# A two-layer decoder trunk: the MLP's down phase in a fixed order, copies of the up seam on two engines, RWKV's v splits and scan load placed anew

## The chip, the cores and the metric

The kernel runs on one core of a Trainium2 chip. Its time is the device time of one execution in microseconds (us); three runs gave 2987.73 us at the median, 2983.43 to 2993.65. A profile is one further execution, recorded instruction by instruction. Engines are named as the profile names them: PE is TensorE (PEld its weight loads), DVE VectorE, ACT ScalarE, POOL GpSimd, SP SyncE, which here only issues transfers; SPq and POOLq are the queues on which SP and POOL issue them.

## What is computed

A trunk of two layers over 1024 tokens of width 1024, all in float32. Each layer has a token mixer (layer 0 a gated linear recurrence, layer 1 RWKV-7), a cross-attention into 256 memory tokens, and an MLP, each between RMS norms and added to the residual:

```python
for i in range(DEPTH):                      # DEPTH = 2
    hn = rms_norm(x, g[0])
    t = rglru_mixer(hn, ...) if i % 2 == 0 else rwkv7_mixer(hn, ...)
    x = x + rms_norm(t, g[1])
    c = mem_cross_attention(rms_norm(x, g[2]), mem_n, c_w_q[i], c_w_kv[i], c_w_o[i])
    x = x + rms_norm(c, g[3])
    m = sqrelu_mlp(rms_norm(x, g[4]), m_w_up[i], m_w_down[i])
    x = x + rms_norm(m, g[5])

def sqrelu_mlp(h, w_up, w_down):            # 1024 -> 4096 -> 1024
    return jnp.square(jax.nn.relu(h @ w_up)) @ w_down
```

In RWKV-7, `v = (x + xx * mu[3]) @ w_rkv[2]`, with `xx` the previous token less this one, is the last of the three large projections ahead of the scan over time; `g = sigmoid(xg @ g1) @ g2` is the gate.

## The kernel before

**Splits.** A float32 matrix enters TensorE as two parts, a high and a low one: ACT casts it (line 217), and DVE, or in places POOL, subtracts the cast from the value (line 218). `mm3` then issues three matmuls for one product: high by high, high by low, low by high (lines 318 to 320). A split of a 128 x 1024 tile is so one ACT and one DVE instruction, and the matmuls with a low operand wait for the second.

**The MLP by seven products.** Both of its multiplications are done in blocks of 2 x 2 with seven block products in place of eight; p1 to p7 are these products, t1 to t4 and s1 to s4 the sums of blocks that enter them.

**The up seam** is the place where the MLP begins. The last of eight token tiles gets its norm (lines 642, 643, 327, 331, 650), and `combine_in` transposes the tokens on TensorE (line 384), four 128 x 128 blocks into a bank of PSUM. ACT copies each bank out with the norm's gain (line 385), 16 copies a layer, in two halves of eight. DVE and POOL then form the sums t1, t2, t3, t4 (lines 405 to 412), and each is split. In `make` (line 449) the w tiles of the first up tiles are loaded and split between the last token tiles; `MAKE` says after which.

**The up phase** (`cphase`) runs over 16 w tiles, two at a time at the start and at the end (`together`). `take` gives out the next split tile of a plan; `depth` says how many are kept split ahead, `ahead` how many more are loaded. For the last tile both are 0. Behind p7 of the last pair the function `then` takes the down phase's first weights and first operands. The result of the up phase goes to DRAM (`spill`), as seven blocks and sums for each of four groups; POOL forms the sums (lines 960 to 963).

**The down phase** has four groups g of 1024 hidden units and seven steps in each, 28 in all. A step multiplies one block or sum of the spilled tokens (A, two tiles of 128 x 1024) with one of the weights (B, two tiles; the sums of these, DSUMS, are formed by POOL at line 445). In each step p goes over four banks with 12 matmuls each (48 a step), after which DVE adds the bank into the accumulator (line 1014), or ACT copies it in group 0. The next group's weights are taken at step 5 (`n == 5`). Where the splits of the next steps stand against these additions on DVE is not written down: `take` emits a split when `depth` allows, and the scheduler places it by its priority.

**RWKV v.** `fphase` goes over eight feature tiles f of v, the first two together. After each, `evac_v` copies v out of PSUM on ACT (line 1425), TensorE transposes it (1435), ACT copies the transposes (1436), and TensorE forms the bonus (1446) and the gate (the product with z). Weights for the next tile are split ahead by `take`. `early(f)` loads what evac_v needs (1459, 1461), and `load(0)`, emitted after f = 6 (`LD`), loads the operands of the scan's first steps (1484, 1488, 1490); the scheduler may issue it earlier. The scan begins with matmuls on v as read back from DRAM (lines 1506 and 1627).

Of the kernel before, what the change touches and what calls it, by code (L numbers as in the profile page):

```python
# [27 lines left out]
MAKE = (5, 6)  # L28
# [21 lines left out]
class Net:  # L50
    def __init__(self, ctx, tc, I, plan=None):
# [3 lines left out]
        self.raws, self.parts, self.rows = {}, {}, {}  # L55
        self.later, self.between = [], []
        self.made = {}
# [31 lines left out]
    @contextmanager  # L89
    def behind(self):  # L90

        with ExitStack() as stack:
            if not self.rec:
                last = {i.engine: i for i in self.nc.cur_bb.bb.instructions}
                for i in last.values():
                    stack.enter_context(self.tc.issue_after(i))
            yield

# [123 lines left out]
    def load(self, desc):  # L222
        kind, w = desc[0], desc[1]
        dma = self.nc.sync.dma_start
        if kind == "d":

            v = w.rearrange("(j e p) (n c) -> e n p j c", e=2, p=128, n=2)
            raw = {}
            for e, n in ((0, 0), (1, 0), (0, 1), (1, 1)):
                raw[e, n] = [self.unit() for _ in range(2)]  # L230
                for i, t in enumerate(raw[e, n]):
                    dma(t.rearrange("p (j c) -> p j c", j=2), v[e, n, :, 2 * i:2 * i + 2, :])
            return raw
        if kind == "a":
            two = [self.unit() for _ in range(2)]
            for i, t in enumerate(two):
                dma(t.rearrange("p (j c) -> p j c", j=2), self.spill[w][:, desc[2], 2 * i:2 * i + 2, :])
            return two
        if kind == "b":
            return None  # L240
# [21 lines left out]
    def take(self, desc):  # L262
        if self.rec:
            self.plan.append(desc)
            return Nothing() if desc[0] in "dab" else (Nothing(), Nothing())
        i = self.taken
        assert self.plan[i][0] == desc[0], (self.plan[i], desc)
        self.taken += 1
        while self.within(i, self.loaded, self.depth + self.ahead):
# [4 lines left out]
        return self.parts.pop(i)  # L274
# [5 lines left out]
    def advance(self, i):  # L280
        while self.split_done < self.loaded and self.within(i, self.split_done, self.depth):
# [5 lines left out]
            elif kind == "d":  # L287
                self.parts[j] = self.rows[self.plan[j][2]] = raw
            elif kind == "a":
                self.parts[j] = [self.split(t) for t in raw]  # L290
            elif kind == "b":
                self.parts[j] = self.combine_d(*self.plan[j][1:])
            else:
                self.parts[j] = self.split(raw)
# [78 lines left out]
    def combine_in(self, xs, hf, g, B):  # L373
# [3 lines left out]
        for k in range(KT):  # L377
# [7 lines left out]
            nc.scalar.activation(t[:, o], p, AF.Copy, scale=self.colt[:, g + k:g + k + 1])  # L385
# [52 lines left out]

    def combine_d(self, name, g):

        f = self.rows[g]
        if name in DSUMS:
            o, x, y = DSUMS[name]
            for i in range(2):
                self.nc.gpsimd.tensor_tensor(f[o][i], f[x][i], f[y][i], ALU.subtract)  # L445
            return [self.split(f[o][0]), self.split(f[o][1], eng=self.nc.gpsimd)]
        return [self.split(t) for t in f[{"b11": (0, 0), "b21": (1, 0), "b22": (1, 1)}[name]]]
# [13 lines left out]
    def cphase(self, w, n, B, func, evac, then, ahead=2):  # L461
# [58 lines left out]
        def together(two, mid=lambda: None):  # L520
            for i in two:
                if i == n - 1:

                    self.depth, self.ahead = 0, 0
                begin(i)
                finish(i)
            mid()
            for step in (p5, p6, p7, p3, p4):
                for i in two:
                    step(*st[i], i)  # L530
                if step is p7 and two[-1] == n - 1:
                    with self.behind():
                        then()
# [405 lines left out]
    def mlp(self, layer, xt, raw, post, late=None):  # L939
# [30 lines left out]
        W = lambda g: self.take(("d", down[g * 1024:g * 1024 + 1024, :], g))  # L970
        ops = []

        def then():

            self.depth, self.ahead = 0, 0
            W(0)
            ops.extend([self.take(("a", 0, 0)), self.take(("b", "b11", 0))])
            self.depth, self.ahead = DOWN

        rest = self.cphase(up, 16, xt, AF.Relu, out, then)  # L980
        acc = self.big((4, 1024))
        raw += [t.rearrange("p t (k c) -> p (t k) c", c=512) for t in acc]
        left, right = slice(0, 512), slice(512, 1024)

# [7 lines left out]
        for g in range(4):  # L992
            if late and g >= LATE:
                late.pop(0)()
            ps = {}
            for n, (name, qa, qb, bank, begins, ends, to) in enumerate(steps):
                if n == 5 and g < 3:
                    W(g + 1)
                A, B = (ops.pop(0), ops.pop(0)) if ops else (self.take(("a", g, qa)), self.take(("b", qb, g)))
                for p in range(4):  # L1000
                    if begins:
                        ps[bank, p] = self.bank(p + 1)
                    o = ps[bank, p]
                    for j in range(4):
                        at = slice((j % 2) * 512 + p * 128, (j % 2) * 512 + p * 128 + 128)
                        bt = slice((j % 2) * 512, (j % 2) * 512 + 512)
                        self.mm3(o, [t[:, at] for t in A[j // 2]], [t[:, bt] for t in B[j // 2]],
                                 begins and j == 0, ends and j == 3, skip_group_check=True)
# [6 lines left out]
                    if g == 3 and name == "p3":  # L1015
                        post(p, acc[0][:, p, :])
                    if g == 3 and name == "p7" and layer == 1 and p == 3:

                        sq = [self.small(1) for _ in range(2)]
# [708 lines left out]
```

## Time and profile before

| what | value |
|---|---|
| median of three runs | 2987.73 us |
| the profiled execution | 2991.93 us, its span 2990.2 us |
| PE busy | 2861.3 us (96% of the span) |
| DVE, ACT, POOL busy | 1812.9, 1355.9, 1166.1 us |
| mean granted TensorE clock | 0.983 of full |
| down phase, layer 0 | about 990 to 1334 us |
| up seams | 702 to 727 and 2353 to 2376 us |
| first v transposes | 1682.49 us |

A row of a timeline gives an instruction's start, its length, the engine, the line, the tiles (written<-read) and in square brackets how long the engine sat idle before it and what ended that. A row of the waits gives the waiting engine and line, what it waited for, the total, how often, and the longest. A row of a table of windows gives the stretch and its length, then the busy time of PE, PEld, DVE, ACT and POOL with the number of instructions, the granted clock (PEclk), the DMA share and GB/s.

### The profile page before, as it was taken

How to read it: one execution, taken by the hardware profiler on the slowest of the kernel's cores; microseconds unless marked ns; L12 is line 12 of the kernel's file. 1: busy time of each engine (PE TensorE's matmuls, PEld its weight loads, DVE VectorE, ACT ScalarE, POOL GpSimd, SP SyncE). 2: the span in 40 equal slices, each digit the busy share in tenths (PEclk: the TensorE clock that was granted, in tenths of full speed). 3: DMA queues.
4: the chain of work that ended last, by engine and by line, in shares of the span. 5: the costliest groups of instructions: out<-in, count | busy, mean ns of one | idle time of the engine just before them, and what ended most of it. 6: DMA issues, size and time to landing. Idle time of an engine off the chain costs nothing. (4 is left out here: it accounts for less than half of the span.)

```text
span 2990.2 us, 42725 instructions
## 1 busy us (share of the span) xinstructions
PE 2861.3 (96%) x16987; PEld 2381.1 (80%) x16987; DVE 1812.9 (61%) x2012; ACT 1355.9 (45%) x1975; POOL 1166.1 (39%) x1055
## 2 busy tenths in 40 slices
PE   7999999999999999999999898989999899999998
PEld 6888798887888878877777677878788788887886
DVE  5576552546455587867685526884354745558776
ACT  6464342536444543347452534442244644454332
POOL 2000110024766664431486215651001566667442
PEclk9999999999999999999999899999999999999999
DMA  8212262113444654332656889752312244455443
GB/s 256 74 50 86 97 200 72 57 71 99 158 155 154 223 201 144 119 113 101 175 163 181 223 246 225 175 131 92 99 53 82 89 147 151 153 210 199 162 137 120
DMA packets 382887, 421.91 MB, mean 141 GB/s; under 512 B 91248, under 2 KB 293216, under 8 KB 382688
## 3 DMA queue, kind: packets, MB, share of 16 engines
q1 hardware_dynamic: 370656, 379.19, 42.1%
q0 software_dynamic: 11568, 39.41, 3.6%
q8 instruction: 133, 2.18, 0.3%
q14 instruction: 66, 0.54, 0.1%
q10 hardware_dynamic: 464, 0.59, 0.1%
HBM read 284.31 MB, written 134.74 MB: 140 GB/s over the span
## 5 line engine op out<-in xcount | busy, mean ns | idle before, releaser
L218 DVE TENSOR_TENSOR u<-u,u 128x1024 fp32r<-128x1024 f32 (+1 forms) x518 | 813.0, 1595 | 366.4 <-ACT u L217 331.7
L217 ACT CAST u<-u 128x1024 fp32r<-128x1024 f32 (+1 forms) x550 | 542.8, 1023 | 372.7 <-PE q L319 139.6
L319 PE MATMUL q<-u,u 128*128 128x512 f32 (+2 forms) x1824 | 699.8, 385 | 12.4 <-DVE u L218 12.1
L318 PE MATMUL q<-u,u 128*128 128x512 f32 (+2 forms) x1824 | 696.6, 386 | 12.9 <-DVE z L1014 8.2
L320 PE MATMUL q<-u,u 128*128 128x512 f32 (+2 forms) x1824 | 694.3, 384 | 1.1 <-DVE u L218 1.1
L318 PE MATMUL p<-u,u 128*128 128x512 f32 (+1 forms) x1728 | 658.6, 384 | 22.7 <-ACT u L217 9.7
L319 PE MATMUL p<-u,u 128*128 128x512 f32 (+1 forms) x1728 | 657.1, 380 | 6.2 <-DVE u L218 6.2
L320 PE MATMUL p<-u,u 128*128 128x512 f32 (+1 forms) x1728 | 656.2, 380 | 3.5 <-DVE u L218 3.5
L329 POOL TENSOR_SCALAR s<-s 128x1 f32<-128x1 f32 x98 | 38.1, 389 | 969.0 <-ACT u L327 949.6
L318 PEld LDWEIGHTS q<-u,u 128*128 128x128 f32 (+1 forms) x1824 | 344.4, 189 | 84.7 <-DVE z L1014 8.8
L319 PEld LDWEIGHTS q<-u,u 128*128 128x128 f32 (+1 forms) x1824 | 344.7, 189 | 82.7 <-DVE u L218 16.2
L318 PEld LDWEIGHTS p<-u,u 128*128 128x128 f32 x1728 | 331.6, 192 | 87.8 <-ACT u L217 14.7
L320 PEld LDWEIGHTS q<-u,u 128*128 128x128 f32 (+1 forms) x1824 | 344.6, 189 | 69.0 <-DVE u L218 2.2
L319 PEld LDWEIGHTS p<-u,u 128*128 128x128 f32 x1728 | 331.8, 192 | 66.8 <-DVE u L218 10.5
L320 PEld LDWEIGHTS p<-u,u 128*128 128x128 f32 x1728 | 331.3, 192 | 65.7 <-DVE u L218 5.2
L445 POOL TENSOR_TENSOR u<-u,u 128x1024 f32<-128x1024 f32 x64 | 181.1, 2851 | 90.5 <-DVE u L218 90.1
L1014 DVE TENSOR_TENSOR z<-z,q 128x512 f32<-128x512 f32 x192 | 129.0, 680 | 84.8 <-PE q L320 84.2
L218 POOL TENSOR_TENSOR u<-u,u 128x1024 fp32r<-128x1024 f32 x32 | 93.8, 2932 | 164.3 <-ACT u L217 112.1
L425 POOL TENSOR_TENSOR u<-u,u 128x512 f32<-128x512 f32 x96 | 152.7, 1596 | 3.1
L960 POOL TENSOR_TENSOR u<-u,u 128x512 f32<-128x512 f32 x32 | 46.3, 1446 | 150.1 <-ACT u L949 137.9
L642 DVE SCALAR_TENSOR_TENSOR u<-p,s,u 128x1024 f32<-128x1024 f32 x24 | 30.8, 1283 | 116.1 <-ACT u L217 78.8
L320 PE MATMUL q<-z,u 128*128 128x512 f32 x256 | 99.5, 390 | 1.1 <-DVE u L218 1.1
(257 smaller groups left out, 3546.3 us busy)
## 6 DMA issues: line engine op xcount, KB each, us to landing
u<-d SPq DMA_DIRECT2D x198, 512.0 KB, 4.6
d<-u SPq DMA_DIRECT2D x109, 512.0 KB, 3.1
d<-u POOLq DMA_DIRECT2D x68, 512.0 KB, 4.1
d<-u SPq DMA_DIRECT2D x132, 256.0 KB, 3.7
u<-in_m_w_up SPq DMA_DIRECT2D x64, 512.0 KB, 5.1
u<-in_m_w_down SPq DMA_DIRECT2D x64, 512.0 KB, 6.3
u<-in_c_w_kv SPq DMA_DIRECT2D x32, 512.0 KB, 6.7
u<-d SPq DMA_DIRECT2D x56, 256.0 KB, 6.1
```

Source lines behind the costliest of these rows:

```text
L217: self.nc.scalar.copy(hv, src)
L218: (eng or self.nc.vector).tensor_tensor(lv, src, hv, ALU.subtract)
L318: mm(o, ah, bh, start=first, stop=False, **kw)
L319: mm(o, ah, bl, start=False, stop=False, **kw)
L320: mm(o, al, bh, start=False, stop=last, **kw)
L329: nc.gpsimd.tensor_scalar(v, ss, 1.0 / n, eps, ALU.mult, ALU.add)
L425: sub = lambda o, x, y: nc.gpsimd.tensor_tensor(o, x, y, ALU.subtract)
L445: self.nc.gpsimd.tensor_tensor(f[o][i], f[x][i], f[y][i], ALU.subtract)
L642: nc.vector.scalar_tensor_tensor(o, src, r, gb, ALU.mult, ALU.mult)
L960: tt(s1, r21, r22, ALU.add)
L1014: nc.vector.tensor_add(to_, to_, o)
```

## The change

Four places are changed.

1. `MAKE` goes from (5, 6) to (4, 5), and in `combine_in` the copies of odd k go to DVE.
2. In `cphase`, the depth before the last two tiles is 2 and 0 (it was the running value, then 0), and `then` becomes two functions: the loads for the down phase come after the operands of the last tile but one, and the first splits behind p7.
3. The down phase's operands no longer go through `take`: at quarter p of step m stands the p-th split of step m + 1, the 12 matmuls, and the addition, and `line("down")` ties these on each engine in the order of the text. POOL's sums stand at the end of the step, for step m + 2. From step 24 on splits stand two steps ahead. The loads of a block are issued two steps ahead.
4. In RWKV's v, the first two feature tiles run with depth 0 and three loads ahead; the splits of later tiles come after f = 1's copy (`behind`). `LD` is 3, with `load(0)` kept at its place in the order, and the load of XTd (line 1490) is a function of its own, after f = 6.

```diff
-MAKE = (5, 6)
+MAKE = (4, 5)
...
+    @contextmanager
+    def line(self, name):
+        with ExitStack() as stack:
+            if not self.rec:
+                last = self.lines.setdefault(name, {})
+                for i in last.values():
+                    stack.enter_context(self.tc.issue_after(i))
...
+                for i in given[n:]:
+                    last[i.engine] = i
...
-            nc.scalar.activation(t[:, o], p, AF.Copy, scale=self.colt[:, g + k:g + k + 1])
+            gc = self.colt[:, g + k:g + k + 1]
+            if k % 2:
+                nc.vector.tensor_scalar(t[:, o], p, gc, None, ALU.mult)
+            else:
+                nc.scalar.activation(t[:, o], p, AF.Copy, scale=gc)
...
-                if i == n - 1:
-                    self.depth, self.ahead = 0, 0
+                if i >= n - 2:
+                    self.depth, self.ahead = 2 * (n - 1 - i), 0
                 begin(i)
                 finish(i)
+                if i == n - 2:
+                    then[0]()
...
-                        then()
+                        then[1]()
...
+        soon = lambda m, turn: [m + 1] if m < turn else [m + 1, m + 2] if m == turn else [m + 2]
+        ps = {}
+        for m, (g, name, qa, qb, bank, begins, ends, to) in enumerate(seq):
+            n = m % 7
...
+            if n == 5 and g < 3:
+                weights(g + 1)
...
+            for i in soon(m, 23):
+                block(i + 1)
+            A, B = ops.pop(m)
+            work = [parts(i) for i in soon(m, 24)]
+            line = lambda: self.line("down")
+            for p in range(4):
+                with line():
+                    for w in work:
+                        w[p]()
...
+                with line():
                     for e, s, new in to:
                         to_ = acc[e][:, p, s]
                         if new and g == 0:
                             nc.scalar.copy(to_, o)
                         else:
                             nc.vector.tensor_add(to_, to_, o)
...
+            with line():
+                for i in soon(m, 23):
+                    sums(i + 1)
...
-LD = 6
+LD = 3
...
         nc.scalar.copy(vt, p)
+        if f == 1:
+            self.depth, self.ahead = DA
+            with self.behind():
+                self.advance(self.taken - 1)
...
+    self.depth, self.ahead = 0, sum(DA)
...
         if fs[-1] == LD:
-            load(0)
+            with self.behind():
+                load(0)
+        if fs[-1] == 6:
+            load_solved(0)
```

Order of DVE in the down phase of layer 0 before, in group 0 (u are operand tiles, z the accumulator, q the banks; L218 is a split's subtraction, L1014 the addition):

```order
L1014 TENSOR_TENSOR z_7611<-z_7611,q_7640 128x512
L218 TENSOR_TENSOR u_8177<-u_8100,u_8176 128x1024
L218 TENSOR_TENSOR u_8181<-u_8101,u_8180 128x1024
L218 TENSOR_TENSOR u_8185<-u_7868,u_8184 128x1024
L1014 TENSOR_TENSOR z_7611<-z_7611,q_7654 128x512
L218 TENSOR_TENSOR u_8189<-u_7869,u_8188 128x1024
L218 TENSOR_TENSOR u_8253<-u_8172,u_8252 128x1024
L218 TENSOR_TENSOR u_8257<-u_8173,u_8256 128x1024
L218 TENSOR_TENSOR u_8263<-u_7864,u_8262 128x1024
```

The same place after (the split's subtraction is L233, the addition L1060):

```order
L233 TENSOR_TENSOR u_8177<-u_8100,u_8176 128x1024
L1060 TENSOR_TENSOR z_7614<-z_7614,q_8180 128x512
L233 TENSOR_TENSOR u_8195<-u_8101,u_8194 128x1024
L1060 TENSOR_TENSOR z_7614<-z_7614,q_8198 128x512
L233 TENSOR_TENSOR u_8213<-u_8016,u_8212 128x1024
L1060 TENSOR_TENSOR z_7614<-z_7614,q_8216 128x512
L233 TENSOR_TENSOR u_8231<-u_8017,u_8230 128x1024
L1060 TENSOR_TENSOR z_7614<-z_7614,q_8234 128x512
```

Runs of three and four splits between two additions became one split between two.

Order of ACT where RWKV's v begins, before (L217 are casts, u_12593 and u_12920 loaded w tiles, L1425 the copy of a v tile, L1436 the copies of its transposes, L1450 the gate):

```order
L217 CAST z_12896<-u_12901 128x1024
L217 CAST u_12922<-u_12593 128x1024
L217 CAST u_12928<-u_12920 128x1024
L1425 COPY u_13030<-p_12932 128x1024
L1436 COPY u_13033<-q_13035 128x8x64
L1436 COPY u_13034<-q_13041 128x8x64
L1450 ACTIVATE u_13047<-q_13051,colt 128x512
L1425 COPY u_13070<-p_12933 128x1024
```

And after (the cast is L232, the copies L1474 and L1490, the gate L1504):

```order
L232 CAST z_12896<-u_12901 128x1024
L1474 COPY u_13022<-p_12924 128x1024
L1490 COPY u_13025<-q_13027 128x8x64
L1490 COPY u_13026<-q_13033 128x8x64
L1504 ACTIVATE u_13039<-q_13043,colt 128x512
L1474 COPY u_13062<-p_12925 128x1024
L232 CAST u_13064<-u_12593 128x1024
L1504 ACTIVATE u_13039<-q_13052,colt 128x512
L1490 COPY u_13025<-q_13073 128x8x64
L1490 COPY u_13026<-q_13081 128x8x64
L232 CAST u_13068<-u_12920 128x1024
```

The casts of both w tiles moved from ahead of the first copy to behind the second, and the second cast behind that tile's own copies.

Order of DVE at the up seam of layer 0 after, from the last token tile's scaling (L645) on (L386 are the copies that ACT had, L408 the sums for t1, L233 the split's subtraction):

```order
L645 TENSOR_SCALAR u_5338<-u_5345,s_5364 128x1024
L471 TENSOR_TENSOR u_5406<-u_5406,q_5405 128x512
L386 TENSOR_SCALAR u_5434<-q_5436,colt 128x512
L408 TENSOR_TENSOR u_5208<-u_5434,u_5208 128x1024
L386 TENSOR_SCALAR u_5447<-q_5449,colt 128x512
L408 TENSOR_TENSOR u_5221<-u_5447,u_5221 128x1024
L386 TENSOR_SCALAR u_5460<-q_5462,colt 128x512
L386 TENSOR_SCALAR u_5473<-q_5475,colt 128x512
L233 TENSOR_TENSOR u_5492<-u_5208,u_5490 128x1024
L233 TENSOR_TENSOR u_5493<-u_5221,u_5491 128x1024
```

Four copies now stand on DVE between the last token tile's scaling and t1's subtractions; before, the two sums alone stood there.

More of the change, by code (lines that the diff above doesn't have):

```diff
@@ L54, in __init__ @@
         self.taken = self.loaded = self.split_done = 0
[L55 removed]
+        self.raws, self.parts = {}, {}
         self.later, self.between = [], []
[L57 removed]
+        self.made, self.lines = {}, {}
         self.depth, self.ahead = 2, 3
@@ L969, in mlp @@
         self.depth, self.ahead = UP
[L970 to L982, printed above, removed]
         left, right = slice(0, 512), slice(512, 1024)
@@ L991, in mlp @@
                  ("p4", 2, "t4", "x", False, True, ((1, left, True),)))
-        for g in range(4):
-            if late and g >= LATE:
-                late.pop(0)()
[L995 to L1008, printed above, removed]
+        seq = [(g, *s) for g in range(4) for s in steps]
@@ new lines, in loads, with first @@
+        def loads():
+            block(0)
+            weights(0)
+            block(1)
+        def first():
+            for work in parts(0):
+                work()
+        rest = self.cphase(up, 16, xt, AF.Relu, out, (loads, first))
+        acc = self.big((4, 1024))
+        raw += [t.rearrange("p t (k c) -> p (t k) c", c=512) for t in acc]
+        soon = lambda m, turn: [m + 1] if m < turn else [m + 1, m + 2] if m == turn else [m + 2]
+        ps = {}
+        for m, (g, name, qa, qb, bank, begins, ends, to) in enumerate(seq):
+            n = m % 7
+            if n == 0 and late and g >= LATE:
+                late.pop(0)()
+            if n == 5 and g < 3:
+                weights(g + 1)
+            if m == len(seq) - 1:
+                self.depth, self.ahead = DOWN
+                self.fetch(self.taken - 1)
+            for i in soon(m, 23):
[7 more added lines that the diff above has]
+                        w[p]()
+                if begins:
+                    ps[bank, p] = self.bank(p + 1)
+                o = ps[bank, p]
+                for j in range(4):
+                    at = slice((j % 2) * 512 + p * 128, (j % 2) * 512 + p * 128 + 128)
+                    bt = slice((j % 2) * 512, (j % 2) * 512 + 512)
+                    self.mm3(o, [t[:, at] for t in A[j // 2]], [t[:, bt] for t in B[j // 2]],
+                             begins and j == 0, ends and j == 3, skip_group_check=True)
+                with line():
```

110 lines of the change are left out of this document (62 added, 48 removed).

## The prediction

> **What bounds the kernel now.** The page's first part comes first, since it tells whether TensorE's work or its waits are to be looked for.
>
> ```profile
> span 2990.2 us, 42725 instructions
> PE 2861.3 (96%) x16987; PEld 2381.1 (80%) x16987; DVE 1812.9 (61%) x2012; ACT 1355.9 (45%) x1975; POOL 1166.1 (39%) x1055
> ```
>
> TensorE is the bound, and no matmul is added or taken away. A timeline of it in the down phase gives its pace:
>
> ```profile
> 999.71 0.39 PE L318 MATMUL q<-u,u 128*128 128x512 f32 x1
> 999.94 0.39 PE L319 MATMUL q<-u,u 128*128 128x512 f32 x1
> ```
>
> Starts are 0.23 us apart; a row's 0.39 us overlaps the next. So time can come only from TensorE's waits and from stretches at half clock. Its waits between the two layers (1360 us), and then in the two up seams (702 and 2353 us, where the transposes open the MLP); the columns are us in total, times, longest:
>
> ```profile
> PE q L359 <- ACT u L1171: 4.4, 1, 4.4
> ...
> PE q L319 <- DVE u L218: 3.2, 3, 1.6
> PE q L384 <- DVE u L650: 1.7, 1, 1.7
> PE q L318 <- ACT u L217: 0.9, 1, 0.9
> ...
> PE q L319 <- DVE u L218: 4.0, 3, 2.5
> PE q L384 <- DVE u L650: 1.7, 1, 1.7
> PE q L318 <- ACT u L217: 1.0, 1, 1.0
> ```
>
> After the first, three rows each are of the seam of layer 0 and of layer 1. A seam holds 5.8 and 6.7 us of waits: the last token tile's scaling (L650), then the cast and subtraction of t1, then of t2 (L217, L218).
>
> **Part 1, up seams.** Half of the 16 copies after the transposes go from ACT to DVE, and the w tiles of the first two up tiles are made a token tile earlier.
>
> ```profile
> 704.46 4.00 PE L384 MATMUL q<-ident,u 128*128 128x128 f32 x17 [1.73 <-DVE u L650]
> ...
> 713.71 0.50 PE L319 MATMUL q<-u,u 128*128 128x512 f32 x1 [1.29 <-DVE u L218]
> ...
> 709.44 1.27 ACT L385 ACTIVATE u<-q,colt 128x512 f32<-128x512 f32 x2 [0.17 <-PE q L384]
> 710.60 1.04 ACT L217 CAST u<-u 128x1024 fp32r<-128x1024 f32 x1
> 711.54 0.69 ACT L385 ACTIVATE u<-q,colt 128x512 f32<-128x512 f32 x1
> ...
> 711.67 5.30 DVE L218 TENSOR_TENSOR u<-u,u 128x1024 fp32r<-128x1024 f32 x2 [1.72 <-ACT u L217]
> ...
> 704.00:708.00 4.00, 3.42 (x15) 2.67 (x16) 2.07 (x3) 2.06 (x3) 0.00 (x0) 0.57 0.00 0
> 708.00:714.00 6.00, 3.37 (x19) 2.07 (x19) 3.70 (x4) 4.99 (x7) 3.80 (x2) 1.00 0.00 0
> 714.00:718.00 4.00, 4.00 (x12) 3.10 (x12) 4.00 (x2) 0.00 (x0) 1.90 (x1) 0.57 0.00 0
> ```
>
> t1's cast at 710.60 stands behind two copies of 0.69 us that another engine could make at the same time; two copies are 1.4, of which the transposes themselves, still at half clock, let about half through: 0.7 off t1's waits. A DVE copy isn't in the trace; L1014 on the same shape (0.67) and L650 (0.75) bound it, so it costs what ACT's does. What DVE takes on there it needs itself: two L218 took 5.30 us beside POOL. So t2's waits (the rest of the L319 rows, 3.2 - 1.29 = 1.9, and 2.7 if t1's is the same in layer 1) go only half: 0.9 and 1.4. Of the 1.7 on L650, a cast of 1.04 leaves the chain, partly covered: 0.7. Layer 0: 0.7 + 0.9 + 0.7 = 2.3; layer 1: 2.8. Clock: 0.57 over 4 us in two windows is some 1.7 us lost in each. The first stays, as the 1.73 shrinks but remains; the second follows the waits on t1, and I take half of it in each layer: 1.7. Sum 6.8, bounds 0 (DVE late by what it took on) and 16.
>
> [...]
>
> **Part 2, last up tile.** Its split is taken a tile earlier. TensorE's waits there, layer 1's (2640 to 2760 us) and layer 0's (988 to 1110):
>
> ```profile
> PE q L318 <- ACT u L217: 0.8, 1, 0.8
> ...
> PE q L318 <- ACT u L217: 0.3, 1, 0.3
> ```
>
> I take 0.8 + 0.3 = 1.1; the split itself lies beside the tile before it, whose matmuls hide it.
>
> **Part 3, down phase.** Waits of TensorE (layer 0 in two rows, then layer 1 in two), the DVE ahead of the first, clocks, and DVE's and POOL's groups over 1100 to 1310 us:
>
> ```profile
> 1091.59 0.80 PE L318 MATMUL q<-u,u 128*128 128x512 f32 x1 [3.88 <-DVE z L1014]
> 1318.48 0.61 PE L319 MATMUL q<-u,u 128*128 128x512 f32 x1 [2.46 <-DVE u L218]
> ...
> 2744.48 0.50 PE L318 MATMUL q<-u,u 128*128 128x512 f32 x1 [3.90 <-DVE z L1014]
> ...
> 2969.04 0.50 PE L319 MATMUL q<-u,u 128*128 128x512 f32 x1 [1.78 <-DVE u L218]
> ...
> 1081.26 9.68 DVE L218 TENSOR_TENSOR u<-u,u 128x1024 fp32r<-128x1024 f32 x3
> 1090.86 0.67 DVE L1014 TENSOR_TENSOR z<-z,q 128x512 f32<-128x512 f32 x1
> ...
> 1093.40:1096.80 3.40, 3.40 (x9) 2.65 (x8) 3.40 (x4) 1.99 (x2) 0.00 (x0) 0.50 0.17 24
> ...
> 1318.00:1322.00 4.00, 3.52 (x9) 2.74 (x10) 4.00 (x6) 1.15 (x2) 1.17 (x1) 0.59 0.42 137
> ...
> L218 DVE TENSOR_TENSOR u<-u,u 128x1024 fp32r<-128x1024 f32 x61 | 92.8, 1542 | 16.6 <-ACT u L217 11.1 <-POOL u L218 4.9 <-PE q L319 0.5
> L1014 DVE TENSOR_TENSOR z<-z,q 128x512 f32<-128x512 f32 x77 | 51.8, 680 | 32.5 <-PE q L320 32.3
> L445 POOL TENSOR_TENSOR u<-u,u 128x1024 f32<-128x1024 f32 x20 | 56.0, 2817 | 35.6 <-DVE u L218 35.2
> ```
>
> The add that frees a bank stood behind three splits of 3.2 us each. With one split ahead of an add at most, it is late by one, and the next step's bank is not needed at once; the 3.88 and 3.90 go. At the end no split is left, which takes 2.46 and 1.78. Together 12.0. Clock: TensorE comes back at 1091.59 at half and stays so to 1096.8, 2.6 lost; around 1318.5 0.41 x 4 = 1.6; layer 1's wait has one such stretch, 1.7 by the same size: 5.9. The gain is 17.9.
>
> What it costs: a quarter of a step is 12 matmuls of 0.227 us = 2.72 us. DVE has there at most one split of 1.54 and one add of 0.68, 2.2, so it fits on the mean; beside POOL 3.2 + 0.7 = 3.9 is 1.2 too long, and a late one is caught up in the next quarters, and the matmuls that need the low half stand 21 or more behind a step's first (4.8 us). The tightest place is the start, where POOL's sums and split for t1 and t2 (2.8 us each, six of them) stand beside the last up tile's own sums: I take 1 us a layer, 0 to 4. At layer 0's end the last token tiles' scaling comes after more of the down phase than before; the 4.4 us wait on L1171 shows how bare that seam is, and I take 0.8 lost (2 gained to 3 lost). Next weights:
>
> ```profile
> u<-in_m_w_down SPq DMA_DIRECT2D x64, 512.0 KB, 6.3
> ```
>
> They are now issued a fixed step ahead, eight of 6.3 us landing overlapped; I put them at nothing, hidden by the 10.9 us of a step. Part 3: 17.9 - 2 - 0.8 = 15.1, bounds 6 and 19.
>
> [...] If all splits met POOL the sum would turn; that is the third rival.
>
> **Part 4, RWKV v and the scan.**
>
> ```profile
> 1682.49 1.97 PE L1435 MATMUL q<-ident,u 128*128 128x128 f32 x8 [11.39 <-ACT u L1425]
> ...
> 1680.36 1.04 ACT L217 CAST u<-u 128x1024 fp32r<-128x1024 f32 x1 [11.99 <-DMA u<-in_b_w_rkv]
> 1681.42 1.01 ACT L1425 COPY u<-p 128x1024 f32<-128x1024 f32 x1
> ...
> 1672.19 9.81 SPq L1488 DMA_DIRECT2D z<-d  x3
> ...
> 1680.00:1684.00 4.00, 1.51 (x7) 1.51 (x8) 1.22 (x1) 2.41 (x3) 1.96 (x3) 0.50 1.17 201
> ...
> 1807.43 0.45 PE L1627 MATMUL q<-u,u 128*64 128x64 f32 x2 [5.24 <-DMA u<-d]
> ```
>
> ACT sat 11.99 us on a cast whose weights were on their way beside the scan's loads (L1488), with the copy that TensorE needs behind it. Both casts now follow v's copies, and the loads are issued later. What remains is a chain: the first copy 1.01, the second 1.01, the cast of f=2's tile 1.04, each with little TensorE work beside it: 3.1, and up to 1 more if the second tile's weights land late; 3.6, bounds 2 and 8. TensorE's order has both tiles' transposes and gate matmuls in that time, so they are not lost but moved. Clock: 0.50 to 1684, so from 1682.49 at least 0.75 lost; I take 0.75. Gain 11.4 - 3.6 + 0.75 = 8.5, bounds 3 and 12. The scan's start waits for L1506, whose place behind the last v tile's stores stays; what goes from the stretch ahead of it are the scan's own loads and a place of w_o's, so that less lies in the queues when it is issued. I take 1.5 of the 5.24, bounds 0 and 4. Part 4: 10.0.
>
> **The sum.** 6.8 + 1.1 + 15.1 + 10.0 = 33.0 off the profiled run's 2991.93 (span 2990.2 and 1.7 around it): 2958.9. That run stands 4.2 above the median of 2987.73, so the median becomes 2955.
>
> **The rivals.** *The waits move on.* Seams are gated by DVE's own splits, which have not got cheaper: up 0, down at its lower bound 6, v and scan 3, last tile 1.1: 10 us, 2978, where over 0.3% (9 us, about what a measurement can tell) is 2978.8. With half of it, 22 us, 2966. For it: the L218 beside POOL in both up seams. Against: the longest four waits have a queue ahead of them that the order shows gone.
>
> *Weights come late.* The next group's eight loads need pool slots that free only step by step, and SP's later blocks, ACT's casts and DVE's fixed line are behind them. At 5 us (under the landing of 6.3) for three groups in two layers, 30 us: 3.0 gained, 2985, no change. Against it: the DMA share in the down phase leaves room (0.42 at 1318).
>
> *Slower: POOL sets DVE's line.* With splits and adds bound in one order, a quarter costs 61/77 of a split and one add. At 1.54 that is 1.9 against 2.72; it decides from a mean split of 2.73, where 0.125 x 224 quarters of both layers = 28 us eat the gain of the rest (17.9) and the 9 us of 0.3%. At 2.9, between the seam's 2.65 and the 3.2 here: 0.26 x 224 = 58 lost, 17.9 gained: 3028. For it: those rows. Against: POOL is busy 56 us of these 210 with L445, and the mean is 1.54 with it. [...]
>
> **How the numbers follow.** Forecast 0.60, waits move on 0.22 (two thirds of it over 0.3%), weights late 0.10, POOL's line 0.08. Faster 0.60 + 0.15 = 0.75; same 0.07 + 0.10 = 0.17; slower 0.08. The forecast's own bounds, 16 + 1 + 19 + 16 = 52 gained at best, give 2936; the upper end takes in the waits that move on and the late weights, 2985. The third rival stays out.
>
> **What would show it.** In the changed profile: no wait on L1014's successor over 1 us in the down phase, splits and adds in turn on DVE, mean split below 2 us; the wait at v's first transposes under 5 us with ACT's copy ahead of the cast; the scan's wait at 3 to 5. Wrong would be: TensorE waits spread over many steps of the down phase; the up seam's L318 and L319 waits as long as before; a wait of DVE on casts that wait for weights.

## The result, and the profile after

The changed kernel is slower: 2996.61 us at the median of 16 runs (2992.20 to 2999.48) against 2987.62 for the kernel before in 16 runs beside them (2980.20 to 2993.65). The ratio is 1.003, with a 95% interval of 1.0022 to 1.0037. The forecast was 2955 us, 33 faster; the time lies above its whole range.

The profiled execution took 2998.47 us. Its page begins so:

```profile
span 2996.8 us, 42733 instructions
PE 2860.6 (95%) x16987; PEld 2376.6 (79%) x16987; DVE 1825.4 (61%) x2028; ACT 1345.0 (45%) x1959; POOL 1152.2 (38%) x1055
```

The matmuls are as many and TensorE's busy time is 0.7 us less; the span is 6.6 longer. So the loss is again in what TensorE waits for. From the list of its waits over the whole span, before and then after:

```profile
PE q L1435 <- ACT u L1425: 12.5, 2, 11.4
PE q L319 <- DVE u L218: 12.1, 9, 2.5
...
PE q L318 <- DVE z L1014: 8.2, 3, 3.9
```

```profile
PE q L318 <- DVE u L233: 24.4, 17, 2.5
...
PE q L1401 <- issue: 6.6, 1, 6.6
```

The two targets of the change are gone from the list: the 11.4 us at v's first transposes (L1435) and the 3.9 us on an addition (L1014), which stood once in each layer. In their place the wait of a low operand on its subtraction (before L319 on L218, after L318 on L233) has doubled, from 12.1 us in 9 places to 24.4 in 17, and a wait of 6.6 us stands at L1401, where none was.

Where the time went is read by taking the k-th matmul of both traces and following how far the second runs behind the first:

| stretch | TensorE after, against before |
|---|---|
| up seams, layer 0 and 1 | 1.1 and 2.5 us gained |
| last up tiles | 0.25 lost, 0.25 gained |
| down phase, layer 0 | 10 lost |
| the seam behind it | 1.3 lost |
| RWKV v | 3 gained |
| start of the scan | 1 lost |
| cross-attention of layer 1 | 3.6 gained, all of it in where half-clock stretches fall |
| down phase, layer 1 | 0.3 lost |
| behind the last matmul | 3.9 lost |

That is 10.45 gained and 16.75 lost, 6.3 of the span's 6.6.

**The down phase of layer 0.** The waits of TensorE from 988 to 1340 us, before, then after:

```profile
PE q L318 <- DVE z L1014: 4.3, 2, 3.9
PE q L319 <- DVE u L218: 2.5, 1, 2.5
```

```profile
PE q L318 <- DVE u L233: 10.5, 7, 2.1
PE q L317 <- DVE z L1060: 2.5, 1, 2.5
PE q L317 <- ACT u L232: 1.2, 1, 1.2
```

Before, two long waits made nearly all of it, 3.9 us on an addition and 2.5 on a subtraction. Now there are seven on a subtraction, six of them of 1.2 to 2.1 us, and one of 2.5 us on an addition. A timeline of the changed kernel, first TensorE, then DVE just ahead, then POOL, shows one of them in the making:

```profile
1071.03 0.50 PE L318 MATMUL q<-u,u 128*128 128x512 f32 x1 [1.20 <-DVE u L233]
...
1065.57 0.69 DVE L1060 TENSOR_TENSOR z<-z,q 128x512 f32<-128x512 f32 x1 [3.63 <-PE q L319]
1066.17 1.47 DVE L233 TENSOR_TENSOR u<-u,u 128x1024 fp32r<-128x1024 f32 x1
1067.56 0.67 DVE L1060 TENSOR_TENSOR z<-z,q 128x512 f32<-128x512 f32 x1
1068.16 2.82 DVE L233 TENSOR_TENSOR u<-u,u 128x1024 fp32r<-128x1024 f32 x1
...
1064.16 5.74 POOL L1000 TENSOR_TENSOR u<-u,u 128x1024 f32<-128x1024 f32 x2
```

DVE stood idle for 3.63 us until TensorE had finished a bank, with the next subtractions behind that addition in its line. Then it had to make two of them and an addition between in a row, both while POOL made two sums (they took 1.47 and 2.82 us, where one took 1.22 alone at 1181.79), and the next step's low operand, which TensorE wanted at 1069.8, was ready at 1071.0. DVE has the time, but it has it before it may use it.

### The profile page after: what moved, and what is told of

Its sections match the earlier page's. It is cut to its first block, busy times and chain, and to the rows that moved or that the text cites. A ratio compares the mean times of both kernels' runs of the same rounds, so it can differ in the third digit from the quotient of the medians.

```text
span 2996.8 us, 42733 instructions
## 1 busy us (share of the span) xinstructions
PE 2860.6 (95%) x16987; PEld 2376.6 (79%) x16987; DVE 1825.4 (61%) x2028; ACT 1345.0 (45%) x1959; POOL 1152.2 (38%) x1055
## 4 chain that ended last, share of the span: by engine, by line
PE 74%; DVE 12%; issue 4%; POOL 3%; ACT 3%; DMA 3%; SPq 2%; DVEq 0%; POOLq 0%; ACTq 0%
PE q L318 13%; PE q L319 13%; PE q L317 13%; PE p L317 10%; PE p L319 10%; PE p L318 10%; DVE u L233 6%; PE q L1595 1%; DVE z L1060 1%; POOL u L1357 1%; ACT u L232 1%; POOL w L1355 1%; DVE u L1154 1%; DMA u<-d 1%; POOL u L1701 1%
## 5 line engine op out<-in xcount | busy, mean ns | idle before, releaser
L233 DVE TENSOR_TENSOR u<-u,u 128x1024 fp32r<-128x1024 f32 (+1 forms) x518 | 826.6, 1613 | 369.3 <-ACT u L232 351.2
L318 PE MATMUL q<-u,u 128*128 128x512 f32 (+2 forms) x1824 | 699.2, 386 | 25.0 <-DVE u L233 24.4
L232 ACT CAST u<-u 128x1024 fp32r<-128x1024 f32 (+1 forms) x550 | 542.1, 1023 | 389.7 <-POOL u L1000 138.3
L319 PE MATMUL q<-u,u 128*128 128x512 f32 (+2 forms) x1824 | 692.1, 384 | 0.5 <-DVE u L233 0.5
L317 PE MATMUL q<-u,u 128*128 128x512 f32 (+2 forms) x1824 | 676.5, 386 | 7.3 <-ACT u L232 2.9
L317 PE MATMUL p<-u,u 128*128 128x512 f32 (+1 forms) x1728 | 659.3, 384 | 20.5 <-ACT u L232 9.7
L318 PE MATMUL p<-u,u 128*128 128x512 f32 (+1 forms) x1728 | 654.9, 379 | 6.6 <-DVE u L233 6.6
L319 PE MATMUL p<-u,u 128*128 128x512 f32 (+1 forms) x1728 | 653.7, 378 | 3.2 <-DVE u L233 3.2
L318 PEld LDWEIGHTS q<-u,u 128*128 128x128 f32 (+1 forms) x1824 | 345.4, 189 | 99.7 <-DVE u L233 33.6
L317 PEld LDWEIGHTS q<-u,u 128*128 128x128 f32 (+1 forms) x1824 | 344.3, 189 | 80.1 <-ACT u L232 5.3
L319 PEld LDWEIGHTS q<-u,u 128*128 128x128 f32 (+1 forms) x1824 | 345.1, 189 | 67.2 <-DVE u L233 0.7
L317 PEld LDWEIGHTS p<-u,u 128*128 128x128 f32 x1728 | 329.9, 191 | 85.4 <-ACT u L232 12.6
L318 PEld LDWEIGHTS p<-u,u 128*128 128x128 f32 x1728 | 330.6, 191 | 68.5 <-DVE u L233 10.8
L319 PEld LDWEIGHTS p<-u,u 128*128 128x128 f32 x1728 | 329.9, 191 | 64.1 <-DVE u L233 4.9
L1000 POOL TENSOR_TENSOR u<-u,u 128x1024 f32<-128x1024 f32 x64 | 187.6, 2948 | 210.7 <-DVE u L233 210.7
L1060 DVE TENSOR_TENSOR z<-z,q 128x512 f32<-128x512 f32 x192 | 128.6, 680 | 104.1 <-PE q L319 104.1
L233 POOL TENSOR_TENSOR u<-u,u 128x1024 fp32r<-128x1024 f32 x32 | 81.8, 2557 | 76.5 <-ACT u L232 75.1
L319 PE MATMUL q<-z,u 128*128 128x512 f32 x256 | 99.8, 390 | 1.2 <-DVE u L233 1.2
L317 PE MATMUL q<-z,u 128*128 128x512 f32 x256 | 99.6, 389 | 0.0
```

The source lines that it names most:

```text
L232: self.nc.scalar.copy(hv, src)
L233: (eng or self.nc.vector).tensor_tensor(lv, src, hv, ALU.subtract)
L317: mm(o, ah, bh, start=first, stop=False, **kw)
L318: mm(o, ah, bl, start=False, stop=False, **kw)
L319: mm(o, al, bh, start=False, stop=last, **kw)
L1060: nc.vector.tensor_add(to_, to_, o)
```

## Experiments

Each ratio is to the kernel before in runs on the same chip. The runs were to tell these theories apart. **H**: the line itself. In split, matmuls, addition, split, each addition waits for TensorE with the next split behind it, so DVE can't use its idle time to get ahead. **D**: DVE has too much work in a quarter, since POOL makes its splits longer, as the third rival had it. **P**: POOL's sums, put at a step's end, come too late. **A1**: work for RWKV (the small weights, "lora": products at L1173, then their casts), which runs in layer 0's down phase only, stands in ACT's line ahead of the down phase's casts. **A2**: splits two steps ahead at the end pile up. And beside these, that parts 1 or 4 lost it.

**Which part?** Each part alone on the kernel before. `x1_up` is part 1:

```diff
-MAKE = (5, 6)
+MAKE = (4, 5)
...
+            if k % 2:
+                nc.vector.tensor_scalar(t[:, o], p, gc, None, ALU.mult)
```

> Only part 1 of the change (w tiles a token tile earlier, odd copies on DVE). Theory A, that each part acts by itself and the down phase is what loses: the two traces differ over the up seams by 1.1 and 2.5 us, so 3 to 4 us faster than before, 2984. Rival B, that the parts gain what was forecast and lose it only together: 7 us faster, 2981. By neither is it slower.

Measured: 2983.79 us, ratio 0.9984 (0.9973 to 0.9995), 6.2 us less than before at the medians. Followed matmul by matmul, its profiled run gains 4.7 us in the two seams, 2.1 and 2.6; it is 7.5 us shorter in all, the rest in stretches that the edit doesn't touch.

`x2_down` is parts 2 and 3, with `then` in two, `soon`, and the line:

```diff
+            for p in range(4):
+                with line():
+                    for w in work:
+                        w[p]()
```

> Only parts 2 and 3 (last up tile's split, down phase in fixed order). Theory A: some 10 us lost in layer 0's down phase, 1 at its end and 4 at the kernel's end, 14 slower than before, 3001. Rival B: 16 us faster, 2972.

Measured: 3004.99 us, ratio 1.0058 (1.0043 to 1.0073).

`x3_v` is part 4:

```diff
-LD = 6
+LD = 3
```

> Only part 4 (RWKV v's splits, the scan's load after f = 3). Theory A: the 11.4 us wait at v's opening falls to under 2, but a wait of 6 to 7 us stands at the merge in f = 5 with a stretch at half clock, and the scan's start loses 1: 2 to 3 us faster, 2985. Rival B: no such wait at the merge, 10 us faster, 2978.

Measured: 2987.90 us, ratio 0.9991 (0.9978 to 1.0004). So parts 2 and 3 lose some 15 us, part 1 gains 6, and part 4 gains almost nothing, 2 us at the medians, and its interval includes no change. All further questions are two: what loses in the down phase, and what ate part 4's gain.

**Is it the fixed order?** `x4_free` is x2 with the text's order but no ties:

```diff
-                for i in last.values():
-                    stack.enter_context(self.tc.issue_after(i))
```

> Parts 2 and 3 with the ties taken out: splits, additions and sums are written in the new order, but no instruction is held behind another by the fixed line, so the scheduler places them as it likes. Theory A, with the ties as the cause: most of the 14 us come back, 2986 to 2992. Theory A', that the order as it is written (splits one step ahead, sums late) is the cause and not the ties: 2998 or more, as with the ties. Rival B: 2972 with or without.

Measured: 2993.27 us, ratio 1.0011 (0.9999 to 1.0023): the ties cost some 12 us. The free order has its own price, at the start of the phase:

```profile
1058.51 0.53 PE L316 MATMUL q<-u,u 128*128 128x512 f32 x1 [3.62 <-DVE u L231]
...
1123.48 0.62 PE L315 MATMUL q<-u,u 128*128 128x512 f32 x1 [4.37 <-DVE z L1054]
```

The second is on an addition, as before's was at 1091.59. `x7_dve` ties DVE's instructions alone:

```diff
-                    last[i.engine] = i
+                    if i.engine == mybir.EngineType.DVE:
+                        last[i.engine] = i
```

> Parts 2 and 3 with only DVE's instructions tied to each other; ACT's casts and POOL's sums go where the scheduler puts them. If DVE's order alone loses (the additions and splits that wait for each other): 3003 as with all ties. If it is the ties on ACT and POOL: 2990 to 2995, as without ties, or better, since DVE then alternates as the change wants.

Measured: 3007.20 us, ratio 1.0061 (1.0046 to 1.0076), as x2. The ties on DVE alone are enough for the loss.

**A1, the small weights.** In the changed kernel ACT, DVE and TensorE show them, the first of two times:

```profile
1176.62 11.47 ACT L232 CAST u<-u 128x1024 fp32r<-128x1024 f32 x12 [25.27 <-DVE u L1173]
...
1172.22 2.50 DVE L1173 TENSOR_TENSOR u<-u,omu 128x512 f32<-128x512 f32 x1
...
1184.79 0.54 PE L318 MATMUL q<-u,u 128*128 128x512 f32 x1 [2.07 <-DVE u L233]
```

The casts of these products came next in ACT's line, and the products came late on DVE, behind its additions. For 25.27 us ACT did nothing, and then had twelve casts to make. `x5_late` is x2 with this work behind the phase:

```diff
-        net.mlp(l, xt, raw, post, [lambda: early.append(rwkv_early(net)), lambda: early.append(rwkv_gate(net))] if l == 0 else None)
+        net.mlp(l, xt, raw, post)
+        if l == 0:
+            early.extend([rwkv_early(net), rwkv_gate(net)])
```

> Parts 2 and 3 with the ties, but the two preparations of RWKV's small weights that layer 0's down phase runs in its groups 2 and 3 are run after the phase. Theory A1, that ACT's casts behind their casts (25 us behind DVE's products) cause layer 0's excess: the waits of 2.1 and 2.0 us near 1184 and 1263 go and with them 4 us or more of layer 0's down phase, while its end may pay for the work moved there; TensorE at the phase's end 4 to 6 us earlier than with parts 2 and 3 alone. Rival A2, that the splits two steps ahead at the end are the larger cause: those two waits go, the 2.5 and 2.2 near 1300 stay, and the phase's end moves by their 4 only if nothing later takes it back.

Measured: 3020.27 us, ratio 1.0103 (1.0088 to 1.0118). At the end of the phase TensorE was some 10 us earlier than in x2, but one wait behind it took more:

```profile
1359.55 0.80 PE L317 MATMUL q<-u,u 128*128 128x512 f32 x1 [29.04 <-ACT u L232]
```

The work has to be somewhere, and the phase is a good place. `x14_lora` is x2 with it cut in two, the products at step 0 and their splits at step 4, in the line:

```diff
-                late.pop(0)()
+                fin = late.pop(0)()
+            if n == 4 and late is not None and g >= LATE:
+                with self.line("down"):
+                    early.append(fin())
...
-    return [self.split(t) for t in (prev, now)]
+    return lambda: [self.split(t) for t in (prev, now)]
```

> Parts 2 and 3 with the ties, but the preparation of RWKV's small weights in layer 0's down phase is cut in two: load and products at step 0 of a group as before, their splits tied into the line at step 4. Theory A1, that ACT's casts wait 25 us in its queue behind casts of these products: as in the run with this work taken out of the phase, the waits of 2.1, 2.0, 2.5 and 2.2 us in layer 0 fall to one of 2, and 8 to 10 us come back without the cost at the phase's end: 2995. Otherwise: 3003 to 3007.

Measured: 2992.90 us, ratio 1.0014 (1.0003 to 1.0024), 12 us less than x2. ACT's longest wait between 1100 and 1345 us is 14.0 us, where x2's are 25.2 and 23.9, and TensorE's waits on the subtraction from 988 to 1345 fall from 10.6 us to:

```profile
PE q L318 <- DVE u L233: 7.2, 6, 2.0
```

Followed matmul by matmul, 9 us are gained in the phase with the seam behind it. Another 5.5 us come at v's opening, which the edit doesn't touch (14.2 us of wait at the first transposes in x2, 9.1 here), and 3.7 were lost ahead of the phase. So A1 is shown, and its size is 9 us.

**A2, two steps ahead.** `x6_one` is x2 with one step ahead throughout:

```diff
-        soon = lambda m, turn: [m + 1] if m < turn else [m + 1, m + 2] if m == turn else [m + 2]
+        soon = lambda m, turn: [m + 1]
```

> Parts 2 and 3 with the ties, but splits one step ahead to the end (none two steps ahead). Theory A2: the waits of 2.5 and 2.2 us near 1300 and the half clock behind them go, 7 to 8 us in layer 0, in place of them a wait of about 2.5 near the end as before the change; 2996 to 2999. Theory A1: no change over 2 us, 3003.

Measured: 3019.36 us, ratio 1.0105 (1.0087 to 1.0123), 14 us more than x2. Splits and the norms of the last tokens now meet at the end of the phase:

```profile
1312.22 1.20 PE L317 MATMUL q<-u,u 128*128 128x512 f32 x4 [2.91 <-ACT u L232]
...
1332.63 0.76 PE L317 MATMUL q<-u,u 128*128 128x512 f32 x1 [3.17 <-DVE z L1056]
1336.41 1.12 PE L358 MATMUL q<-ident,u 128*128 128x128 f32 x4 [3.02 <-DVE u L641]
```

A2 fell, and so did the expectation that by A1 nothing changes: this piece of the change is worth 14 us as it is.

**P and D, POOL and the load of DVE.** `x9_sums` is x2 with POOL's sums at the start of step m, not at its end:

```diff
+            with line():
+                for i in soon(m, 23):
+                    sums(i + 1)
             for p in range(4):
```

> Parts 2 and 3 with the ties, but POOL's two sums for step m + 2 at the start of step m in place of its end. Theory P, that POOL's sums are late and hold ACT's cast, which holds DVE's split, which holds TensorE (the waits of 1.3, 1.2, 1.6 and 2.0 us that both layers have): three of the four go in each layer, 8 us less, 2997. Theory D, that DVE's own line is too slow beside POOL and the sums only sit in it: the waits stay within 2 us in total, 3003 to 3005, or move to the step before.

Measured: 3029.39 us, ratio 1.0139 (1.0123 to 1.0154). It tells nothing of P: the sum is written over a block that an earlier step has still to split, so here that split comes behind the sum and takes the sum in place of the block. The added dependence is likely to be what makes it slower, which was not tried by itself, and of P this run shows nothing.

`x12_dvesplit` is x2 with the splits that POOL makes for the DSUMS given to DVE, which adds to DVE's work:

```diff
-                        for t, e in zip(fs, (None, nc.gpsimd if name in DSUMS else None))]
+                        for t, e in zip(fs, (None, None))]
```

> Parts 2 and 3 with the ties, but the one split in four that POOL makes in the steps with sums goes to DVE: POOL has some 2.4 to 3 us less in each of 16 steps of a layer, DVE 1.2 more. Theory P: the waits of 1.2 and 1.6 go and the time falls by 3 us or more. Theory D: DVE is later still, 5 us or more slower, 3010.

Measured: 3014.27 us, ratio 1.0086 (1.0071 to 1.0101), 9 more than x2, as D expected and P did not: POOL has less to do here, and no gain came. It doesn't exclude P, since DVE has more to do at the same time. DVE's line is the tight one, whatever makes it so. From 1100 to 1310 us its groups in the changed kernel:

```profile
L233 DVE TENSOR_TENSOR u<-u,u 128x1024 fp32r<-128x1024 f32 x69 | 124.9, 1819 | 2.4 <-ACT u L232 2.4
L1060 DVE TENSOR_TENSOR z<-z,q 128x512 f32<-128x512 f32 x71 | 47.8, 680 | 34.0 <-PE q L319 34.0
```

Before, the mean split was 1.54 us (the rows of L218 and L1014 in the prediction); it is 1.82 now. But 34.0 us of 210 DVE still sat waiting for TensorE, so its load as such is not what is short.

**H, the addition ahead of the split.** `x13_lag` is x2 with the same instructions, each addition (in group 0 also ACT's copies, at the end the norms that follow) one quarter later, behind the next quarter's split in the line:

```diff
+        ps, held, sq = {}, [], None
...
                with line():
                    for w in work:
                        w[p]()
+                if held:
+                    held.pop()()
...
-                with line():
-                    for e, s, new in to:
+                def end(p=p, o=o, g=g, name=name, to=to):
+                    with line():
+                        for e, s, new in to:
...
+                held.append(end)
+        held.pop()()
```

> Parts 2 and 3 with the ties, but each addition stands one quarter later in the line: DVE makes the next split before the addition that waits for TensorE. Theory H, that the line loses because DVE waits for TensorE at each addition (3 us and more at a step's first) with the next split behind it, and the splits beside POOL (2.8 us) can then not catch up: the four common waits go in both layers, 10 to 14 us less than with parts 2 and 3 alone, 2992; DVE's wait at the addition falls. [...]

Measured: 2973.99 us, ratio 0.9948 (0.9928 to 0.9967): 31 us less than x2 from moving each addition past one split, two to three times the 10 to 14 that H expected. The subtraction is late seven times from 988 to 1340 us in the changed kernel (10.5 us, above). What DVE's additions waited for there:

```profile
DVE z L1060 <- PE q L319: 51.6, 20, 4.6
```

and both in x13:

```profile
PE q L318 <- DVE u L233: 3.1, 2, 2.5
...
DVE z L1060 <- PE q L319: 33.3, 35, 2.2
```

The additions wait more often and shorter, 33.3 us in place of 51.6, and the subtraction is late twice, not seven times. The mean split from 1100 to 1310 us is the same in both (x13's row):

```profile
L233 DVE TENSOR_TENSOR u<-u,u 128x1024 fp32r<-128x1024 f32 x68 | 122.6, 1811 | 2.4 <-ACT u L232 2.4
```

So H holds, and D falls, and with it that POOL's lengthening of the splits alone makes them late. P loses ground too: ACT's casts waited on POOL's sums for 51.9 us from 988 to 1345 us in the changed kernel, and in x13 they still do for 41.2. Followed matmul by matmul against x2, the profiled run of x13 gains 16 us in the down phase of layer 0, 4 in the seam behind it, 8 in that of layer 1, and 3 behind the last matmul, 31 together. Of the 16, 12 come in groups 1 to 3, where DVE makes every addition, so it isn't ACT's copies of group 0 that do it. `x15_both` adds x14's edit to x13:

> Both of these. If H and A1 hold and add, the down phase loses nothing or gains as forecast: 2980 to 2986, faster than before. If one of them is not the cause, no better than the better of the two.

Measured: 2972.12 us, ratio 0.9945 (0.9924 to 0.9965), 2 less than x13 with overlapping intervals, not the 12 that the edit gave on x2. Two things stand behind that. The two waits of 2 us that the small weights caused in x2 are gone in x13 already, and of what the edit gave in the phase 3.4 us are left. And those are lost again at v's first transposes, which neither edit touches; TensorE's wait there in x13, then in x15:

```profile
PE q L1487 <- ACT u L1477: 8.9, 1, 8.9
PE q L1490 <- ACT u L1480: 13.8, 1, 13.8
```

This wait was 11.4 us before, 14.2 in x2, 9.1 in x14, 8.9 in x13 and 13.8 in x15, all without part 4, so differences of up to 5 us between them can come from there.

**What ate part 4's gain.** The changed kernel at v: two waits of TensorE where the 11.39 was, then SP's queue, ACT and TensorE 70 us later, the scan's start, and two windows (PE, PEld, DVE, ACT, POOL, granted clock, DMA share, GB/s):

```profile
1680.12 1.09 PE L1489 MATMUL q<-ident,u 128*128 128x128 f32 x8 [0.43 <-ACT u L1474]
1682.06 1.10 PE L1500 MATMUL q<-u,ones 128*128 128x512 f32 x2 [0.84 <-DVE w L1355]
...
1743.14 6.27 SPq L1542 DMA_DIRECT2D z<-d  x4
...
1753.06 0.59 SPq L248 DMA_DIRECT2D u<-in_b_w_rkv  x1
...
1766.46 1.04 ACT L232 CAST u<-u 128x1024 fp32r<-128x1024 f32 x1 [13.96 <-DMA u<-in_b_w_rkv]
...
1769.71 0.28 PE L1401 MATMUL q<-u,u 32*32 32x32 f32 x2 [6.59 <-issue]
...
1815.74 0.45 PE L1692 MATMUL q<-u,u 128*64 128x64 f32 x2 [6.82 <-DMA u<-d]
...
1764.00:1770.00 6.00, 0.28 (x2) 0.18 (x2) 3.34 (x4) 3.49 (x5) 0.00 (x0) 0.61 0.58 140
1770.00:1776.00 6.00, 5.74 (x74) 4.60 (x75) 1.63 (x3) 2.54 (x5) 0.57 (x1) 0.53 0.80 254
```

The opening is won. But with `LD` at 3 the scan's loads (L1542) stand in SP's queue ahead of the w tile's (L248), ACT waits 13.96 us for that tile, and the copies for the merge's matmuls (L1401) are behind the cast: what stood at f = 0 before now stands at f = 5. Half clock follows, 0.61 and 0.53 in the two windows. `x8_v5` is x3 with the loads two tiles later:

```diff
-LD = 3
+LD = 5
```

> Part 4 alone with the scan's load after f = 5 in place of f = 3, so that the weights of the last v tiles are ahead of it in SP's queue. Theory A: the opening wait stays gone and the wait of 6 to 7 us at the merge goes; 8 to 11 us faster than before, 2980, if the scan's start doesn't wait longer than 7. If the merge's wait is not from the weights' place in the queue, it stays: 2987.

Measured: 2984.22 us, ratio 0.9986 (0.9976 to 0.9995). In x3's own profile the merge waits 3.5 us, not the 6 to 7 expected, and the scan's start 7.4. In x8 the wait at the merge is gone; two are left, one on a copy behind a cast whose w_o tile was on its way, one at the scan's start:

```profile
PE q L1643 <- DMA u<-d: 5.3, 1, 5.3
PE q L1440 <- ACT u L1425: 3.5, 1, 3.5
```

The gain on x3 is 3.7 us at the medians, 1.5 by the ratios, and their intervals overlap: that the wait goes with the load's place is shown, what it is worth is not. `x11_after5` is the whole change with this edit:

> The whole change with the scan's load after f = 5 in place of f = 3. By the parts, 3 to 4 us of the changed kernel's loss come back (2993), and the loss against before that remains is the down phase's.

Measured: 2993.36 us, ratio 1.0014 (1.0005 to 1.0024), 3.3 below the changed kernel.

**The best of it.** `x10_best` is parts 1 and 4 with `LD` 5, the down phase as before:

> Part 1 and part 4 with the scan's load after f = 5, without parts 2 and 3: the two pieces that gained by themselves. If they add, 6.2 + 4.4 = 10.6 us faster than before: 2978. If the one takes what the other gained, 2982.

Measured: 2978.09 us, ratio 0.9964 (0.9951 to 0.9977), as expected if the two gains add. `x16_all` is the whole change with `LD` 5, the later additions and the small weights in two:

> The whole change with the scan's load after f = 5, the addition one quarter later and the small weights' splits at step 4. With the parts' gains of 6 and 4 us: 2970 to 2976 if the down phase is mended; 2985 or more if it is not.

Measured: 2958.07 us, ratio 0.9900 (0.9885 to 0.9916), 32 us below the kernel before, and the fastest of all, 12 below what was expected. Part of that is v's opening, where 13.8 us in x15 have become 0.4 and 0.8, with 4.4 on a later copy. It has the same matmuls:

```profile
span 2956.7 us, 42735 instructions
PE 2844.7 (96%) x16987; PEld 2370.4 (80%) x16987; DVE 1828.2 (62%) x2028; ACT 1346.4 (46%) x1959; POOL 1158.8 (39%) x1055
```

## Why the prediction was wrong

**Part 1, up seams: near in the sum, with luck, and not in its terms.** 6.8 was forecast; x1 gained 6.2 at the medians (4.8 by the ratio, 1.5 to 8.1 by its interval), and 4.7 where the seams themselves are followed. Within the changed kernel it was 3.6. The 1.73 on the last token tile's scaling went, though 2 us of short waits on the copies came, and t1's wait on its subtraction grew from 1.29 to 2.17 us behind the copies that DVE took on, which the forecast feared for t2, while that on its cast shrank from 0.9 to 0.3:

```profile
711.16 0.79 PE L318 MATMUL q<-u,u 128*128 128x512 f32 x1 [2.17 <-DVE u L233]
```

Of the two half-clock stretches the forecast kept the first. It is the first that went: x1's windows have full clock where the transposes are (0.57 before), and half behind them.

```profile
702.00:710.00 8.00, 4.67 (x30) 3.28 (x30) 6.53 (x8) 4.60 (x6) 2.08 (x1) 1.00 0.00 0
710.00:716.00 6.00, 4.58 (x11) 3.62 (x12) 6.00 (x4) 0.16 (x1) 3.70 (x3) 0.56 0.00 0
```

**Part 2, last up tile: wrong, and small.** 1.1 was forecast, nothing came: one wait of 1.18 on a cast (990.11 us; the row of L317 on L232 above) took the place of two short ones.

**Part 3, down phase: wrong; this decided the case.** 15.1 gained was forecast; parts 2 and 3 alone lost 15. The step that failed is "it fits on the mean", with "a late one is caught up in the next quarters". The waits it counted as gone are gone, and the two-step lead does what was said at the end (14 us by x6). But in this line, which alternates, idle time can't be carried over. In the changed kernel DVE reaches an addition early, waits for TensorE with the next split behind it, and when a split of 2.8 us comes there is no lead to spend. The sum added durations per quarter, 1.54 + 0.68 against 2.72, where it had to ask for each instruction when it may start, and what stands behind it. x13 shows it: same instructions, same mean split (1.81 us), one place later. Against the kernel before, followed matmul by matmul, it gains 9 us in layer 0's phase with its seam, and 8 in layer 1's with the end: 17, where 15.1 were forecast, and its ratio gives 15.5. So the waits were worth what the forecast put down for them. The wrong term is the price of the order behind the phase's start, which it put at nothing; x13 against x2 puts it at 31 us.

A second step failed with it: at layer 0's phase nothing was put down for the small weights, which lie in it (their products, L1124, stand in before's groups of DVE). They make the difference between the two layers, 10 us lost against 0.3; x14 shows 9 us of it. On x13 the same edit was worth 3.4 in the phase, so the small weights hurt a line without lead the most.

A third is the end: the norms' instructions on DVE now stand ahead of the last addition. Before, then after:

```profile
2980.72 0.68 DVE L1014 TENSOR_TENSOR z<-z,q 128x512 f32<-128x512 f32 x1
```

```profile
2984.39 1.22 DVE L638 TENSOR_TENSOR u<-u,u 128x1024 f32<-128x1024 f32 x1
2985.52 0.68 DVE L1060 TENSOR_TENSOR z<-z,q 128x512 f32<-128x512 f32 x1
```

That is the 3.9 us behind the last matmul. It was not tried alone; in x13, which moves the norms with the additions, 3 of it are gone.

**Part 4, RWKV v and the scan: right in the opening, wrong in what follows.** 8.5 at the opening were forecast; some 11 came, since 0.43 and 0.84 us are left where 3.6 were put down. But "the loads are issued later" was taken as free: the one queue that the loads were moved within, SP's, was not followed to the next tile's weights. The new stall with its half clock took 8 of it back. The scan's start, 1.5 gained by the forecast, lost 1 to 1.6: the wait is 6.82 us against 5.24.

**The rivals.** "POOL sets DVE's line" had the sign, the engine and the place right, and its mechanism wrong. By its own condition (a mean split over 2.73 us) it could not come, at 1.82: even with the 69 splits to 71 additions of the changed kernel, 69/71 x 1.82 + 0.68 is 2.45 us a quarter, under 2.72, and DVE had 34 us idle in the stretch. What it and the forecast shared is the mean. "Weights come late" did not come: no wait of TensorE in the down phase ends on a transfer. "The waits move on" describes part 4, and half of part 3. The forecast's own test spoke: it called "TensorE waits spread over many steps of the down phase" the sign that it was wrong, and that is what the page of the changed kernel shows.

**The sum.** The parts alone give -6.2 + 15 - 2.1 = 6.7 us, against 9 measured at the medians; by the ratios it is -4.8 + 17.3 - 2.7 = 9.8. The differences lie within what the intervals leave open. Open stay what the free order (x4) would give with a remedy for the start of the phase, theory P, and what sets the length of the wait at v's first transposes where part 4 is not applied.

## What to carry to other kernels

Where a fixed order makes an engine alternate between work that waits for TensorE and work that TensorE waits for, put the second first; here a lead of one split was worth 31 us. Sums of durations per step don't show this, and a fixed order takes away the freedom that hid it. When a load is moved, follow the queue that it is moved into to the next transfer that somebody waits for. And before an engine's line is fixed for a phase, list everything else that runs on it in that phase.

## What the runs showed of the hardware

Whether a wait of TensorE is followed by half clock is not told by its length. Beside the 2.07 us at 1184.79 above stand two more waits of the changed kernel's down phases; the windows are those behind the three:

```profile
1265.10 0.50 PE L318 MATMUL q<-u,u 128*128 128x512 f32 x1 [2.00 <-DVE u L233]
2949.37 0.50 PE L318 MATMUL q<-u,u 128*128 128x512 f32 x1 [1.94 <-DVE u L233]
...
1185.00:1188.00 3.00, 3.00 (x8) 2.40 (x8) 3.00 (x4) 3.00 (x4) 1.73 (x1) 0.52 0.48 195
1265.00:1268.00 3.00, 2.90 (x13) 2.41 (x14) 3.00 (x5) 3.00 (x4) 1.32 (x1) 1.00 0.72 294
2949.30:2952.00 2.70, 2.63 (x7) 2.12 (x8) 2.70 (x4) 0.00 (x0) 0.00 (x0) 0.59 0.03 6
```

2.07 and 1.94 us were followed by half clock, 2.00 was not. The half-clock stretch cost some 1.7 us more each time: matmuls 0.43 apart, not 0.23. One and the same wait tells it best: in the cross-attention of layer 1 both kernels have 2.05 us on a cast, at 2192.33 us before and at 2199.33 in the changed kernel. Behind it the granted clock was 0.50 before (2194 to 2199 us) and 1.00 after (2200.5 to 2205.5). What decides whether half clock follows, these rows don't show.

The same kernel's runs spread over 7 us (2992.20 to 2999.48), and whole stretches without any edit moved by 3.6 us with the place of half-clock stretches; so parts worth less than 5 us can't be read from one profile.

A subtraction of 128 x 1024 took 1.22 us alone (at 1181.79 us) and 2.82 beside POOL's sum (at 1068.16), an addition from PSUM 0.67 to 0.69 in both. It was not what decided: x13 won its 31 us over x2 with a mean split of 1.81 us, where x2 has 1.83 (both from 1100 to 1310 us). A sum of POOL got longer too: of the two from 1064.16 us on, the first took 2.39 us, and the second, which began while a subtraction ran, 3.39.
